# Strided attention on one core: casts, transposes, exps and masked values for two groups at a time

## Chip, cores, metric

One core of one Trainium2 chip. The metric is the device time of one execution in microseconds (us). Times inside a profile count from the start of its span, which is some 1.7 us shorter than the timed execution. A run over 1.5% above the fastest of its kernel counts as slow here, and ratios use the other runs ("fast") alone.

## The reference

Every query attends to the 16 keys at positions 0, 64, 128 and so on.

```python
batch, heads, seq, dim = (8, 12, 1024, 64)      # Q, K, V in float32; stride 64
attend_positions = np.arange(0, seq, stride)    # 16 positions, the same for every query
scores  = np.einsum('bhqd,bhkd->bhqk', q, k) * scale       # scale = 1/sqrt(dim)
weights = np.exp(scores - max); weights /= weights.sum() + 1e-10
result  = np.einsum('bhqk,bhkd->bhqd', weights, v)
```

Q and the result are 25.2 MB each. Only a sixteenth of K and V is read (0.39 MB each).

## The kernel before

The 96 heads form 24 groups of 4. A group's way: load Q (1024 KB), cast it to bf16 on GpSimd (POOL), transpose it on VectorE (DVE), four score matmuls on TensorE (PE), two exps on ScalarE (ACT), then eight output matmuls in three tiles of 3, 2 and 3. DVE takes the reciprocal of the sums of each tile. It also multiplies tiles 0 and 2; ACT copies tile 1 and POOL multiplies it. At last the group is stored (1024 KB). All loads and stores are issued to one queue (q1 of the page: 51.12 of 51.19 MB) in program order. In the timelines every engine starts its instructions in program order, and in the traces all 50 transfers land in the order of their issue. In the names below, qn is a loaded Q tile, qb its bf16 copy, qt the transposed copy, sc the scores, w the exps, v the masked values and o_ps the outputs in PSUM; "lead" is how many groups ahead of its outputs a step runs.

```python
QBUFS = 8; OBUFS = 9
# qb, qt, rec, score tile (1 bank), output tile (3 banks): 2 buffers each
def cast(g):      nc.gpsimd.tensor_copy(out=qb[g], in_=qn[g])                    # 128x2048
def transpose(g): nc.vector.transpose(qt[g].bitcast(I32), qb[g].bitcast(I32))
def scores(g):    # four matmuls into one bank, then two exps into w_bufs[g % 3]
    ...
def outputs(g, c):
    i0, n = ((0, 3), (3, 2), (5, 3))[c]
    ...           # n matmuls, then:
    nc.vector.reciprocal(r, ps[:, 0:n, 4 * D : 4 * D + 4])
    if n == 3:
        nc.vector.tensor_tensor(out=to, in0=o, in1=by, op=ALU.mult)
    else:
        nc.scalar.copy(to, o)
        nc.gpsimd.tensor_tensor(out=to, in0=to, in1=by, op=ALU.mult)
...
def ahead(g):
    transpose(g + 2); scores(g + 1); values(g + 2); cast(g + 3)     # limits at NG cut

for g in range(NG):
    if g > 0:
        ahead(g)              # the work of later groups stands before the outputs of g
    for c in range(3):
        outputs(g, c)
    if g == 0:
        ahead(g)
    ...                       # keys and values of later groups
    store(g)
    if g + QBUFS < NG:
        load(g + QBUFS)
```

So a cast runs three groups ahead of its outputs, a transpose two and the scores one.

The softmax here doesn't subtract the row's maximum and nothing guards it: scores larger than these inputs give would overflow.

Of the kernel before, what the change touches and what calls it, by code (L numbers as in the profile page):

```python
# [11 lines left out]
FP32 = mybir.dt.float32  # L12
BF16 = mybir.dt.bfloat16
I16 = mybir.dt.int16
I32 = mybir.dt.int32
# [4 lines left out]
def _ap_with(ap: bass.AP, new_ap, extra_offset: int = 0) -> bass.AP:  # L20
    return dataclasses.replace(
        ap, ap=[list(p) for p in new_ap], offset=ap.offset + extra_offset
    )


def _copy(nc, out: bass.AP, in_: bass.AP):

    sides = [
        mybir.BassSymbolicTensorAccessPattern(
            ap=side.ap, dtype=side.dtype, bass_ap=side,  # L30
            is_dma=True, for_custom_bir_dma=True,
        )
        for side in (in_, out)
    ]
    return nc.sync.add_instruction(  # L35
        mybir.InstDMACopy(
            name=nc.get_next_instruction_name(), engine=mybir.EngineType.SP,
            ins=sides[:1], outs=sides[1:], queue="qSPDynamicHW",
            mode="Copy",
        )  # L40
    )
# [5 lines left out]



@with_exitstack  # L50
def kernel(
    ctx: ExitStack,
# [7 lines left out]
    nc = tc.nc  # L60

    B, H, S, D = Q.shape
    NK = S // stride
    scale = 1.0 / math.sqrt(D)

    P = 128
    HG = 4
    NG = B * H // HG
    NC = NG // 2
    SD = S * D  # L70
    KW = P + NK
    assert B * H == NG * HG and S == 1024 and D == 64 and NK == 16
    QBUFS = 8
    OBUFS = 9

    const = ctx.enter_context(tc.tile_pool(name="const", bufs=1))
    qn_pool = ctx.enter_context(tc.tile_pool(name="qn", bufs=QBUFS))
    out_pool = ctx.enter_context(tc.tile_pool(name="outsb", bufs=OBUFS))
    qb_pool = ctx.enter_context(tc.tile_pool(name="qb", bufs=2))
    qt_pool = ctx.enter_context(tc.tile_pool(name="qt", bufs=2))  # L80
    rec_pool = ctx.enter_context(tc.tile_pool(name="rec", bufs=2))
    psum_sc = ctx.enter_context(tc.tile_pool(name="psc", bufs=2, space=bass.MemoryType.PSUM))
    psum_o = ctx.enter_context(tc.tile_pool(name="po", bufs=2, space=bass.MemoryType.PSUM))

    ctx.enter_context(tc.manual_schedule())
# [5 lines left out]
    qn = {}  # L91

    def load(g):
        qn[g] = qn_pool.tile([P, 32 * D], FP32, name="qn", tag="qn")
        n = P if g < 2 else 32
        _copy(nc, qn[g], _ap_with(Q, [[HG * SD // n, n], [1, HG * SD // n]], g * HG * SD))

    nc.sync.dma_start(k_raw, _ap_with(K, kv_src))
    load(0)
    nc.sync.dma_start(v_raw, _ap_with(V, kv_src))  # L100
    for g in range(1, QBUFS):
        load(g)


# [2 lines left out]
    id_v = identity.rearrange("p (c b a k) -> p c b a k", c=2, b=2, a=2)  # L107
# [5 lines left out]
    col4 = const.tile([P, 4], I16, name="col4")  # L113
    nc.gpsimd.iota(col4, pattern=[[1, 4]], base=0, channel_multiplier=0)
    for c in range(2):
        for a in range(2):
            for e in range(2):
                nc.gpsimd.tensor_copy(  # L118
                    out=perm_v[:, c, a, :, e], in_=id_v[:, c, :, a]
                )  # L120

    k_t = const.tile([P, NG, 2, KW], BF16, name="k_t")
    nc.vector.memset(k_t[:, 0:8], 0.0)  # L123
    w_bufs = []
    for i in range(3):
        w = const.tile([P, 8, P], BF16, name=f"w{i}")
        nc.vector.memset(w, 0.0)  # L127
        w_bufs.append(w)
    nc.gpsimd.memset(k_t[:, 8:NG], 0.0)  # L129
# [10 lines left out]
        out=s_sel, in0=col4, scalar1=slot_f, scalar2=None, op0=ALU.is_equal  # L140
    )
    v_bufs = []
    for i in range(3):
        v = const.tile([P, 4 * D + 4], BF16, name=f"v{i}")
        nc.vector.tensor_copy(out=v[:, 4 * D :], in_=s_sel)
        v_bufs.append(v)
    mask = const.tile([P, 4, D], BF16, name="mask")
    nc.vector.tensor_copy(out=mask, in_=s_sel.unsqueeze(2).to_broadcast([P, 4, D]))
# [7 lines left out]
    def key_rows(m):  # L156
        part = slice(4 * m, 4 * m + 4)
        nc.scalar.copy(k_bf[:, part], k_raw[:, part])  # L158
        nc.vector.transpose(  # L159
            k_r[:, part].rearrange("p n d -> p (n d)").bitcast(I32),  # L160
            k_bf[:, part].rearrange("p n d -> p (n d)").bitcast(I32),
        )
# [12 lines left out]


    def value_rows(n):
        for c in range(2):
            vp = psum_sc.tile([P, NC // 2, D], FP32, name="vp", tag="sc")
            nc.tensor.matmul(  # L180
                vp, lhsT=perm_v[:, c].rearrange("p a b e k -> p (a b e k)"),
                rhs=v_bf[:, 6 * n : 6 * n + 6], start=True, stop=True,
            )
            nc.vector.tensor_copy(out=v_rep[:, 6 * n : 6 * n + 6, c], in_=vp)  # L184

    qb, qt, wt, vb, rec, out_sb = {}, {}, {}, {}, {}, {}


    def values(g):
        vb[g] = v_bufs[g % 3]  # L190
        nc.gpsimd.tensor_tensor(  # L191
            out=vb[g][:, 0 : 4 * D].rearrange("p (s d) -> p s d", s=4), in0=mask,
            in1=v_rep[:, g // 2, g % 2].unsqueeze(1).to_broadcast([P, 4, D]),
            op=ALU.mult,
        )

    def cast(g):
        qb[g] = qb_pool.tile([P, 32 * D], BF16, name="qb", tag="qb")
        nc.gpsimd.tensor_copy(out=qb[g], in_=qn[g])  # L199

    def transpose(g):
        qt[g] = qt_pool.tile([P, 32 * D], BF16, name="qt", tag="qt")
        nc.vector.transpose(qt[g].bitcast(I32), qb[g].bitcast(I32))  # L203

    def scores(g):
        sc = psum_sc.tile([P, 512], FP32, name="sc", tag="sc")
        q = qt[g]
        for e in range(2):
            for f in range(2):
                nc.tensor.matmul(  # L210
                    sc, lhsT=k_t[:, g, f, NK * (1 - e) : NK * (1 - e) + P],
                    rhs=_ap_with(
                        q, [q.ap[0], [D, 8], [16 * D, 2], [2, 32]],
                        extra_offset=8 * D * e + f,
                    ),
                    start=e + f == 0, stop=e + f == 2,
                )
        w = wt[g] = w_bufs[g % 3]
        for a in range(2):
            wa = w[64 * a : 64 * a + 64]  # L220
            nc.scalar.activation(  # L221
                out=_ap_with(wa, [wa.ap[0], [P, 8], [1, 2], [2, 32]], extra_offset=64 * a),
                in_=sc[64 * a : 64 * a + 64].rearrange("p (t x q) -> p t x q", t=8, x=2),
                func=AF.Exp, bias=0.0, scale=scale,
            )


    def outputs(g, c):
        if c == 0:
            out_sb[g] = out_pool.tile([P, 4, 8, D], FP32, name="out_sb", tag="out_sb")  # L230
            rec[g] = rec_pool.tile([P, 8, 4], FP32, name="rec", tag="rec")
        i0, n = ((0, 3), (3, 2), (5, 3))[c]
        ps = psum_o.tile([P, 3, 512], FP32, name="o_ps", tag="o")
        for i in range(n):
            nc.tensor.matmul(  # L235
                ps[:, i, 0 : 4 * D + 4], lhsT=wt[g][:, i0 + i], rhs=vb[g],
                start=True, stop=True,
            )
        r = rec[g][:, i0 : i0 + n]
        o = ps[:, 0:n, 0 : 4 * D].rearrange("p i (s d) -> p i s d", s=4)  # L240
        to = out_sb[g][:, :, i0 : i0 + n].rearrange("p s i d -> p i s d")
        by = r.unsqueeze(3).to_broadcast([P, n, 4, D])
        nc.vector.reciprocal(r, ps[:, 0:n, 4 * D : 4 * D + 4])  # L243
        if n == 3:
            nc.vector.tensor_tensor(out=to, in0=o, in1=by, op=ALU.mult)  # L245
        else:
            nc.scalar.copy(to, o)  # L247
            nc.gpsimd.tensor_tensor(out=to, in0=to, in1=by, op=ALU.mult)  # L248

    def store(g):  # L250
        o = out_sb[g]
        _copy(
            nc,
            _ap_with(out, [[16 * D, P], [2 * SD, 2], [1, 16 * D]], g * HG * SD),
            _ap_with(o, [o.ap[0], [1, 1], [1, 32 * D]]),
        )

    key_rows(0)
    cast(0)
    cast(1)  # L260
    keys(0, 0)
    transpose(0)
    scores(0)
    keys(0, 1)
    nc.vector.tensor_copy(out=v_bf, in_=v_raw)
    transpose(1)
    value_rows(0)
    values(0)
    values(1)
    cast(2)  # L270
    def ahead(g):
        if g + 2 < NG:
            transpose(g + 2)
        if g + 1 < NG:
            scores(g + 1)
        if g + 2 < NG:
            values(g + 2)
        if g + 3 < NG:
            cast(g + 3)

    for g in range(NG):
        if g > 0:
            ahead(g)
        for c in range(3):
            outputs(g, c)
        if g == 0:
            ahead(g)
        if g in (1, 5):
            key_rows(g // 4 + 1)
        if g in (2, 3, 6, 7):  # L290
            keys(g // 4 + 1, g % 4 - 2)
        if g == 4:
            value_rows(1)
        store(g)
        if g + QBUFS < NG:
            load(g + QBUFS)
# [1 line left out]
_INS = ['Q', 'K', 'V', 'stride']  # L298
_OUTS = [((8, 12, 1024, 64), 'float32')]
# [30 lines left out]
```

## Time and profile before

| | before |
|---|---|
| time, median of 3 | 129.21 us (129.09 to 131.93, a slow run) |
| span of the profiled run | 127.6 us |
| DMA queue busy | 96.7% of the span |
| DVE, POOL, PE, ACT busy | 75%, 71%, 53%, 45% |
| last store issued | 119.9 us |

The rows of digits in the prediction below are the page's slices: the span in 40 equal parts, busy share in tenths. Lines such as "20.57 0.63 SPq ..." are DMA issues: start, duration, and what is moved. Lines of groups end with "busy us, mean ns of one | idle time of the engine before them and who ended it". "Half clock" (also "cold") names what the traces show: four score matmuls take 1.86 to 1.92 us instead of 1.06, and the granted clock in the traces' records is 0.5 instead of 1. These records begin at 24.8 us before and at 29.9 us in the changed kernel; ahead of that the PEclk row and the means over a stretch count a full clock that nothing measured.

### The profile page before, as it was taken

The page shows a single profiled execution, that of the slowest core. Times are in us where ns is not written, and L with a number is a line of the kernel's source. Part 1 is how long each engine was busy: PE and PEld are TensorE (multiplying, and loading weights), DVE is VectorE, ACT ScalarE, POOL GpSimd, SP SyncE. Part 2 cuts the span into 40 slices and gives each one's busy share as a digit, 9 for nine tenths or more (in the row PEclk, how much of TensorE's full clock was granted, in tenths as well). Part 3 has the DMA queues.
Part 4 walks back from the last instruction along what each step waited for, and adds up shares of the span by engine and source line. Part 5 has one row for each costly group of instructions (what it writes and reads, how often), then busy time and mean ns, then how long its engine had stood idle before and what let it go on. Part 6 is the DMA issues. An engine that isn't in the chain of part 4 may idle for free.

```text
span 127.6 us, 1150 instructions
## 1 busy us (share of the span) xinstructions
PE 67.2 (53%) x292; PEld 30.1 (24%) x292; DVE 95.5 (75%) x167; ACT 57.5 (45%) x96; POOL 90.3 (71%) x89
## 2 busy tenths in 40 slices
PE   0005267766456796436757565379734877365100
PEld 0002032233222343212423232124221433132000
DVE  6947557788898678898879888897889878977300
ACT  4110614576771458776445653543554626462100
POOL 8962489877898286898888888898689887433300
PEclk9999999999955558999756999955999657998555
DMA  2999989898998998999989989999999999999980
GB/s 68 378 319 468 462 360 483 349 483 362 460 465 352 480 455 339 506 385 393 501 344 447 460 375 450 426 403 457 442 380 455 439 393 421 424 426 424 429 360 26
DMA packets 7910, 51.19 MB, mean 401 GB/s; under 512 B 3872, under 2 KB 3872, under 8 KB 3872
## 3 DMA queue, kind: packets, MB, share of 16 engines
q1 hardware_dynamic: 7904, 51.12, 96.7%
q8 instruction: 2, 0.03, 0.1%
q14 instruction: 4, 0.03, 0.1%
HBM read 25.95 MB, written 25.17 MB: 401 GB/s over the span
## 4 chain that ended last, share of the span: by engine, by line
DVE 48%; DMA 16%; PE 14%; issue 9%; POOL 4%; SPq 1%; ACT 0%; DVEq 0%; POOLq 0%
DVE out_sb L245 30%; PE o_ps L235 11%; DVE qt L203 10%; DMA out_dram<-out_sb 9%; DMA qn<-in_Q_dram 7%; DVE rec L243 7%; PE sc L210 3%; POOL out_sb L248 2%; POOL qb L199 1%; DVE v_rep L184 1%; SPq L35 1%; POOL v L191 1%; ACT out_sb L247 0%; SPq L100 0%; DVE k_r L159 0%
## 5 line engine op out<-in xcount | busy, mean ns | idle before, releaser
L235 PE MATMUL o_ps<-v,w 128*128 128x260 bf16 x192 | 40.0, 333 | 36.1 <-DVE out_sb L245 34.5
L221 ACT ACTIVATE w<-sc 64x512 bf16<-64x512 f32 x48 | 35.3, 735 | 30.1 <-PE sc L210 28.3
L199 POOL CAST qb<-qn 128x2048 bf16<-128x2048 f32 x24 | 45.3, 1889 | 4.2 <-DMA qn<-in_Q_dram 4.2
L245 DVE TENSOR_TENSOR out_sb<-o_ps,rec 128x768 f32<-128x768 f32 x48 | 46.0, 958 | 1.7
L248 POOL TENSOR_TENSOR out_sb<-out_sb,rec 128x512 f32<-128x512 f32 x24 | 25.0, 1042 | 22.2 <-ACT out_sb L247 22.2
L210 PE MATMUL sc<-qt,k_t 128*128 128x512 bf16 x96 | 33.3, 479 | 12.8 <-DVE qt L203 11.6
L235 PEld LDWEIGHTS <-w 128*128 128x128 bf16 x192 | 18.7, 113 | 63.5 <-DVE out_sb L245 48.1
L203 DVE STREAM_TRANSPOSE qt<-qb 128x1024 int32<-128x1024 int32 x24 | 29.6, 1233 | 4.7 <-POOL qb L199 4.7
L243 DVE RECIPROCAL rec<-o_ps 128x12 f32<-128x12 f32 (+1 forms) x72 | 15.3, 212 | 15.9 <-PE o_ps L235 15.8
L247 ACT COPY out_sb<-o_ps 128x512 f32<-128x512 f32 x24 | 14.0, 585 | 24.9 <-DVE rec L243 12.1
L191 POOL TENSOR_TENSOR v<-mask,v_rep 128x256 bf16<-128x256 bf16 x24 | 16.0, 669 | 2.3 <-DVE v_rep L184 2.3
L210 PEld LDWEIGHTS <-k_t 128*128 128x128 bf16 x96 | 10.8, 113 | 23.8 <-issue 10.7
L169 ACT COPY k_t<-k_r 32x128 bf16<-32x128 bf16 x20 | 5.9, 295 | 2.2 <-DVE k_r L159 1.9
L129 POOL MEMSET k_t<- 128x4608 bf16 x1 | 3.9, 3937 | 0.0
L180 PE MATMUL vp<-v_bf,perm_v 128*128 128x384 bf16 x4 | 1.8, 513 | 2.4 <-DVE v_rep L184 2.4
L139 DVE TENSOR_SCALAR s_sel<-col,slot_f 128x4 bf16<-128x4 int16 x1 | 2.5, 2546 | 0.1
L158 ACT CAST k_bf<-k_raw 128x256 bf16<-128x256 f32 x3 | 1.2, 405 | 3.1 <-DMA k_raw<-in_K_dram 3.0
L184 DVE CAST v_rep<-vp 128x384 bf16<-128x384 f32 x4 | 2.1, 543 | 0.6 <-PE vp L180 0.6
L123 DVE MEMSET k_t<- 128x1152 uint32 x1 | 1.0, 1018 | 1.0 <-PEq L311 1.0
L158 ACT ACT_TABLE_LOAD x1 | 1.3, 1283 | 0.7 <-PEq L311 0.7
L127 DVE MEMSET w<- 128x512 uint32 x3 | 1.5, 485 | 0.2
L118 POOL COPY perm_v<-identity 128x32 bf16<-128x32 bf16 x8 | 1.2, 209 | 0.0
(16 smaller groups left out, 5.0 us busy)
## 6 DMA issues: line engine op xcount, KB each, us to landing
qn<-in_Q_dram SPq DMA_DIRECT2D x24, 1024.0 KB, 11.7
out_dram<-out_sb SPq DMA_DIRECT2D x24, 1024.0 KB, 9.8
k_raw<-in_K_dram SPq DMA_DIRECT2D x1, 384.0 KB, 4.3
v_raw<-in_V_dram SPq DMA_DIRECT2D x1, 384.0 KB, 7.3
```

Source lines behind the costliest of these rows:

```text
L129: nc.gpsimd.memset(k_t[:, 8:NG], 0.0)
L169: op(k_t[dst : dst + 32, 8 * m + c : 8 * m + 8 : 2, :, col : col + NK], k_r[src : src + 32, 4 * m : 4 * m + 4].rearrange("p n (a k f) -> p ...
L191: nc.gpsimd.tensor_tensor(out=vb[g][:, 0 : 4 * D].rearrange("p (s d) -> p s d", s=4), in0=mask, in1=v_rep[:, g // 2, g % 2].unsqueeze(1).t ...
L199: nc.gpsimd.tensor_copy(out=qb[g], in_=qn[g])
L203: nc.vector.transpose(qt[g].bitcast(I32), qb[g].bitcast(I32))
L210: nc.tensor.matmul(sc, lhsT=k_t[:, g, f, NK * (1 - e) : NK * (1 - e) + P], rhs=_ap_with(q, [q.ap[0], [D, 8], [16 * D, 2], [2, 32]], extra_ ...
L221: nc.scalar.activation(out=_ap_with(wa, [wa.ap[0], [P, 8], [1, 2], [2, 32]], extra_offset=64 * a), in_=sc[64 * a : 64 * a + 64].rearrange( ...
L235: nc.tensor.matmul(ps[:, i, 0 : 4 * D + 4], lhsT=wt[g][:, i0 + i], rhs=vb[g], start=True, stop=True,)
L243: nc.vector.reciprocal(r, ps[:, 0:n, 4 * D : 4 * D + 4])
L245: nc.vector.tensor_tensor(out=to, in0=o, in1=by, op=ALU.mult)
L247: nc.scalar.copy(to, o)
L248: nc.gpsimd.tensor_tensor(out=to, in0=to, in1=by, op=ALU.mult)
```

## The change

The intent is to pay the fixed part of an instruction once for two groups (170 ns of a transpose, by the 303 ns for 128 columns and 1233 for 1024 in the trace of before). A pair's Q tile is 128x4096. One cast, one transpose, one masked-values multiply and two exps serve both groups, and the score tile has two banks, one for each group. To start early, the first three pairs go group by group. In exchange there are five Q pairs (ten loads up front), eight output tiles, one qb pair and one score tile.

```diff
-    QBUFS = 8
-    OBUFS = 9
+    QBUFS = 5          # pairs
+    OBUFS = 8
-    qb_pool ... bufs=2          psum_sc ... bufs=2
+    qb_pool ... bufs=1          psum_sc ... bufs=1     (tiles of two groups)
...
+    def cast(n, h=slice(0, 2)):
+        ...
+        nc.gpsimd.tensor_copy(out=qb[n][:, h], in_=qn[n][:, h])
...
     for n in range(NC):
         g = 2 * n
         outputs(g, 0)
         outputs(g, 1)
+        if n == 0:
+            transpose(1, one)
+            group_weights(2)            # scores and exps of one group
+            values(1)
+            cast(1, two)
+        ...                             # n == 1 alike
+        elif 2 < n < NC - 1:
+            scores(g + 2)
+            scores(g + 3)
+            weights(n + 1)              # exps of a pair
+            if n + 2 < NC:
+                transpose(n + 2)
+            if n + 3 < NC:
+                cast(n + 3)
         outputs(g, 2)
         store(g)
+        if n == 2:
+            transpose(3)
+            scores(6)
+            scores(7)
+            weights(3)
+            cast(4)
         outputs(g + 1, 0)
         ...
         store(g + 1)
+        if n == 2:
+            transpose(4)
+            cast(5)
+        if n + 2 < NC:
+            values(n + 2)
```

The work for later groups now stands in the middle of a group's outputs, and from pair 3 on a cast runs three pairs ahead and a transpose two.

More of the change, by code (lines that the diff above doesn't have):

```diff
@@ L70 @@
     SD = S * D
+    QW = 32 * D
+    VW = 4 * D + 4
     KW = P + NK
     assert B * H == NG * HG and S == 1024 and D == 64 and NK == 16
-    QBUFS = 8
-    OBUFS = 9
+    QBUFS = 5
+    OBUFS = 8
     const = ctx.enter_context(tc.tile_pool(name="const", bufs=1))
@@ L78 @@
     out_pool = ctx.enter_context(tc.tile_pool(name="outsb", bufs=OBUFS))
-    qb_pool = ctx.enter_context(tc.tile_pool(name="qb", bufs=2))
+    qb_pool = ctx.enter_context(tc.tile_pool(name="qb", bufs=1))
     qt_pool = ctx.enter_context(tc.tile_pool(name="qt", bufs=2))
-    rec_pool = ctx.enter_context(tc.tile_pool(name="rec", bufs=2))
-    psum_sc = ctx.enter_context(tc.tile_pool(name="psc", bufs=2, space=bass.MemoryType.PSUM))
+    rec_pool = ctx.enter_context(tc.tile_pool(name="rec", bufs=4))
+    psum_sc = ctx.enter_context(tc.tile_pool(name="psc", bufs=1, space=bass.MemoryType.PSUM))
     psum_o = ctx.enter_context(tc.tile_pool(name="po", bufs=2, space=bass.MemoryType.PSUM))
@@ L93, in load @@
     def load(g):
-        qn[g] = qn_pool.tile([P, 32 * D], FP32, name="qn", tag="qn")
+        if g % 2 == 0:
+            qn[g // 2] = qn_pool.tile([P, 2, QW], FP32, name="qn", tag="qn")
         n = P if g < 2 else 32
-        _copy(nc, qn[g], _ap_with(Q, [[HG * SD // n, n], [1, HG * SD // n]], g * HG * SD))
+        _copy(
+            nc, qn[g // 2][:, g % 2],
+            _ap_with(Q, [[HG * SD // n, n], [1, HG * SD // n]], g * HG * SD),
+        )
     nc.sync.dma_start(k_raw, _ap_with(K, kv_src))
@@ L100 @@
     nc.sync.dma_start(v_raw, _ap_with(V, kv_src))
-    for g in range(1, QBUFS):
+    for g in range(1, 2 * QBUFS):
         load(g)
@@ L115 @@
     for c in range(2):
-        for a in range(2):
-            for e in range(2):
-                nc.gpsimd.tensor_copy(
-                    out=perm_v[:, c, a, :, e], in_=id_v[:, c, :, a]
-                )
+        for e in range(2):
+            nc.gpsimd.tensor_copy(
+                out=perm_v[:, c, :, :, e],
+                in_=id_v[:, c].rearrange("p b a k -> p a b k"),
+            )
     k_t = const.tile([P, NG, 2, KW], BF16, name="k_t")
@@ L124 @@
     w_bufs = []
-    for i in range(3):
-        w = const.tile([P, 8, P], BF16, name=f"w{i}")
+    for i in range(2):
+        w = const.tile([P, 16, P], BF16, name=f"w{i}")
         nc.vector.memset(w, 0.0)
@@ L142 @@
     v_bufs = []
-    for i in range(3):
-        v = const.tile([P, 4 * D + 4], BF16, name=f"v{i}")
-        nc.vector.tensor_copy(out=v[:, 4 * D :], in_=s_sel)
+    for i in range(2):
+        v = const.tile([P, 2, VW], BF16, name=f"v{i}")
+        nc.vector.tensor_copy(
+            out=v[:, :, 4 * D :], in_=s_sel.unsqueeze(1).to_broadcast([P, 2, 4])
+        )
         v_bufs.append(v)
@@ L177, in value_rows @@
     def value_rows(n):
+        vp = psum_o.tile([P, 3, 512], FP32, name="vp", tag="o")
+        part = slice(6 * n, 6 * n + 6)
         for c in range(2):
-            vp = psum_sc.tile([P, NC // 2, D], FP32, name="vp", tag="sc")
             nc.tensor.matmul(
-                vp, lhsT=perm_v[:, c].rearrange("p a b e k -> p (a b e k)"),
-                rhs=v_bf[:, 6 * n : 6 * n + 6], start=True, stop=True,
-            )
-            nc.vector.tensor_copy(out=v_rep[:, 6 * n : 6 * n + 6, c], in_=vp)
@@ L186 @@
-    qb, qt, wt, vb, rec, out_sb = {}, {}, {}, {}, {}, {}
-    def values(g):
-        vb[g] = v_bufs[g % 3]
+                vp[:, c, 0 : 6 * D], lhsT=perm_v[:, c].rearrange("p a b e k -> p (a b e k)"),
+                rhs=v_bf[:, part], start=True, stop=True,
+            )
+        nc.vector.tensor_copy(
+            out=v_rep[:, part].rearrange("p n c d -> p c n d"),
+            in_=vp[:, 0:2, 0 : 6 * D].rearrange("p c (n d) -> p c n d", n=6),
+        )
+    qb, qt, wt, vb, sc, rec, out_sb = {}, {}, {}, {}, {}, {}, {}
@@ L191, in values @@
+    def values(n):
+        vb[n] = v_bufs[n % 2]
         nc.gpsimd.tensor_tensor(
-            out=vb[g][:, 0 : 4 * D].rearrange("p (s d) -> p s d", s=4), in0=mask,
-            in1=v_rep[:, g // 2, g % 2].unsqueeze(1).to_broadcast([P, 4, D]),
+            out=vb[n][:, :, 0 : 4 * D].rearrange("p h (s d) -> p h s d", s=4),
+            in0=mask.unsqueeze(1).to_broadcast([P, 2, 4, D]),
+            in1=v_rep[:, n].unsqueeze(2).to_broadcast([P, 2, 4, D]),
             op=ALU.mult,
         )
-    def cast(g):
-        qb[g] = qb_pool.tile([P, 32 * D], BF16, name="qb", tag="qb")
-        nc.gpsimd.tensor_copy(out=qb[g], in_=qn[g])
@@ L201, in transpose @@
-    def transpose(g):
-        qt[g] = qt_pool.tile([P, 32 * D], BF16, name="qt", tag="qt")
-        nc.vector.transpose(qt[g].bitcast(I32), qb[g].bitcast(I32))
+    def cast(n, h=slice(0, 2)):
+        if n not in qb:
+            qb[n] = qb_pool.tile([P, 2, QW], BF16, name="qb", tag="qb")
+        nc.gpsimd.tensor_copy(out=qb[n][:, h], in_=qn[n][:, h])
+    def transpose(n, h=slice(0, 2)):
+        if n not in qt:
+            qt[n] = qt_pool.tile([P, 2, QW], BF16, name="qt", tag="qt")
+        nc.vector.transpose(
+            qt[n][:, h].rearrange("p h d -> p (h d)").bitcast(I32),
+            qb[n][:, h].rearrange("p h d -> p (h d)").bitcast(I32),
+        )
@@ L205, in scores @@
     def scores(g):
-        sc = psum_sc.tile([P, 512], FP32, name="sc", tag="sc")
-        q = qt[g]
+        n, h = divmod(g, 2)
+        if h == 0:
+            sc[n] = psum_sc.tile([P, 2, 512], FP32, name="sc", tag="sc")
+        q = qt[n]
         for e in range(2):
@@ L210, in scores @@
                 nc.tensor.matmul(
-                    sc, lhsT=k_t[:, g, f, NK * (1 - e) : NK * (1 - e) + P],
+                    sc[n][:, h], lhsT=k_t[:, g, f, NK * (1 - e) : NK * (1 - e) + P],
                     rhs=_ap_with(
                         q, [q.ap[0], [D, 8], [16 * D, 2], [2, 32]],
-                        extra_offset=8 * D * e + f,
+                        extra_offset=h * QW + 8 * D * e + f,
                     ),
@@ L217, in scores, with weights @@
                 )
-        w = wt[g] = w_bufs[g % 3]
+    def weights(n, h0=0, hn=2):
+        w = wt[n] = w_bufs[n % 2]
         for a in range(2):
@@ L221, in scores @@
             nc.scalar.activation(
-                out=_ap_with(wa, [wa.ap[0], [P, 8], [1, 2], [2, 32]], extra_offset=64 * a),
-                in_=sc[64 * a : 64 * a + 64].rearrange("p (t x q) -> p t x q", t=8, x=2),
+                out=_ap_with(
+                    wa, [wa.ap[0], [P, 8 * hn], [1, 2], [2, 32]],
+                    extra_offset=64 * a + 8 * P * h0,
+                ),
+                in_=sc[n][64 * a : 64 * a + 64, h0 : h0 + hn].rearrange(
+                    "p h (t x q) -> p (h t) x q", t=8, x=2
+                ),
                 func=AF.Exp, bias=0.0, scale=scale,
@@ L228, in outputs @@
     def outputs(g, c):
+        n, h = divmod(g, 2)
         if c == 0:
@@ L231, in outputs @@
             rec[g] = rec_pool.tile([P, 8, 4], FP32, name="rec", tag="rec")
-        i0, n = ((0, 3), (3, 2), (5, 3))[c]
+        i0, m = ((0, 3), (3, 2), (5, 3))[c]
         ps = psum_o.tile([P, 3, 512], FP32, name="o_ps", tag="o")
-        for i in range(n):
+        for i in range(m):
             nc.tensor.matmul(
-                ps[:, i, 0 : 4 * D + 4], lhsT=wt[g][:, i0 + i], rhs=vb[g],
+                ps[:, i, 0:VW], lhsT=wt[n][:, 8 * h + i0 + i], rhs=vb[n][:, h],
                 start=True, stop=True,
             )
-        r = rec[g][:, i0 : i0 + n]
-        o = ps[:, 0:n, 0 : 4 * D].rearrange("p i (s d) -> p i s d", s=4)
-        to = out_sb[g][:, :, i0 : i0 + n].rearrange("p s i d -> p i s d")
-        by = r.unsqueeze(3).to_broadcast([P, n, 4, D])
-        nc.vector.reciprocal(r, ps[:, 0:n, 4 * D : 4 * D + 4])
-        if n == 3:
+        r = rec[g][:, i0 : i0 + m]
+        o = ps[:, 0:m, 0 : 4 * D].rearrange("p i (s d) -> p i s d", s=4)
+        to = out_sb[g][:, :, i0 : i0 + m].rearrange("p s i d -> p i s d")
+        by = r.unsqueeze(3).to_broadcast([P, m, 4, D])
+        nc.vector.reciprocal(r, ps[:, 0:m, 4 * D : VW])
+        if m == 3:
             nc.vector.tensor_tensor(out=to, in0=o, in1=by, op=ALU.mult)
@@ L254, in store, with group_weights @@
             _ap_with(out, [[16 * D, P], [2 * SD, 2], [1, 16 * D]], g * HG * SD),
-            _ap_with(o, [o.ap[0], [1, 1], [1, 32 * D]]),
+            _ap_with(o, [o.ap[0], [1, 1], [1, QW]]),
         )
+        if g + 2 * QBUFS < NG:
+            load(g + 2 * QBUFS)
+    def group_weights(g):
+        scores(g)
+        weights(g // 2, g % 2, 1)
+    one, two = slice(0, 1), slice(1, 2)
     key_rows(0)
-    cast(0)
-    cast(1)
     keys(0, 0)
-    transpose(0)
-    scores(0)
+    cast(0, one)
@@ L264 @@
+    transpose(0, one)
     keys(0, 1)
+    group_weights(0)
+    cast(0, two)
     nc.vector.tensor_copy(out=v_bf, in_=v_raw)
-    transpose(1)
     value_rows(0)
     values(0)
-    values(1)
-    cast(2)
-    def ahead(g):
-        if g + 2 < NG:
-            transpose(g + 2)
-        if g + 1 < NG:
-            scores(g + 1)
-        if g + 2 < NG:
-            values(g + 2)
-        if g + 3 < NG:
-            cast(g + 3)
-    for g in range(NG):
-        if g > 0:
-            ahead(g)
-        for c in range(3):
-            outputs(g, c)
-        if g == 0:
-            ahead(g)
-        if g in (1, 5):
-            key_rows(g // 4 + 1)
-        if g in (2, 3, 6, 7):
-            keys(g // 4 + 1, g % 4 - 2)
-        if g == 4:
+    transpose(0, two)
@@ new lines @@
+    group_weights(1)
+    cast(1, one)
+    for n in range(NC):
+        g = 2 * n
+        outputs(g, 0)
+        outputs(g, 1)
+        if n == 0:
[3 more added lines that the diff above has]
+            cast(1, two)
+        elif n == 1:
+            transpose(2, one)
+            group_weights(4)
+            cast(2, two)
+        elif 2 < n < NC - 1:
[6 more added lines that the diff above has]
+                cast(n + 3)
+        outputs(g, 2)
+        store(g)
+        if n == 2:
[4 more added lines that the diff above has]
+            cast(4)
+        outputs(g + 1, 0)
+        outputs(g + 1, 1)
+        if n == 0:
+            transpose(1, two)
+            group_weights(3)
+            cast(2, one)
+        elif n == 1:
+            transpose(2, two)
+            group_weights(5)
+            cast(3)
+        outputs(g + 1, 2)
+        store(g + 1)
+        if n == 2:
[3 more added lines that the diff above has]
+            values(n + 2)
+        if n in (0, 4):
+            key_rows(n // 4 + 1)
+        if n in (1, 2, 5, 6):
+            keys(n // 4 + 1, n % 4 - 1)
+        if n == 2:
@@ L293 @@
             value_rows(1)
-        store(g)
-        if g + QBUFS < NG:
-            load(g + QBUFS)
 _INS = ['Q', 'K', 'V', 'stride']
```

## The prediction

> **What bounds the kernel now.** I read the page's slices and queue line first.
>
> ```profile
> DVE  6947557788898678898879888897889878977300
> ...
> POOL 8962489877898286898888888898689887433300
> PEclk9999999999955558999756999955999657998555
> DMA  2999989898998998999989989999999999999980
> ...
> q1 hardware_dynamic: 7904, 51.12, 96.7%
> ```
>
> The reader is to see that the DMA row is full from the second slice to the last but one, while no compute row is. The queue was busy 96.7% of 127.6 us = 123.4 us; only 4.2 us are free, at the two ends. The bytes don't change, so 123.4 us plus those ends is a floor: nothing in this change can win 2%.
>
> Then the busy time by stretch, because the totals hide how near the compute is to this floor (columns: us, busy us and instructions of each engine, clock, DMA share, GB/s).
>
> ```profile
> 25.20:62.00 36.80, 22.02 (x103) 10.25 (x104) 30.23 (x55) 22.32 (x43) 28.02 (x24) 0.81 1.00 422
> 62.00:99.00 37.00, 22.98 (x106) 10.52 (x104) 31.81 (x54) 17.95 (x27) 31.39 (x27) 0.82 1.01 428
> 99.00:120.00 21.00, 12.81 (x59) 5.69 (x59) 16.77 (x30) 9.38 (x14) 12.04 (x12) 0.77 1.01 424
> ```
>
> DMA is saturated in all three, at about 424 GB/s: a 1024 KB transfer costs 2.47 us, a group (load and store) 4.94 us.
>
> The DMA issues in order of time say how far ahead of that the compute is:
>
> ```profile
> 20.57 0.63 SPq L35 DMA_DIRECT2D out_dram<-out_sb  x1
> ...
> 27.36 0.59 SPq L35 DMA_DIRECT2D out_dram<-out_sb  x1
> ...
> 46.58 0.59 SPq L35 DMA_DIRECT2D out_dram<-out_sb  x1
> ...
> 92.61 27.79 SPq L35 DMA_DIRECT2D out_dram<-out_sb  x8
> ```
>
> These are stores 0, 1, 5, and 16 to 23 (the last issued at 119.9 in the view of the output tensor). Ledger: by 9.6 us the slices' rates (68, 378, 319 GB/s over 3.2 us each) make 2.45 MB, of which K and V are 0.79. The rest of eight loads, 6.7 MB, takes till 25.5 us. Allowing some 0.5 us for issue (my choice), store g must be issued by 25 + 4.94 g up to g = 16, later ones 2.47 us apart: store 23 by 121.3. It came at 119.9. **So DMA bounds it, but compute has 1.4 us of slack at the end**; between, up to 11 us (store 16: 92.6 against 104).
>
> [...] the transposes agree: 303 ns for 128 columns, 1233 for 1024, so 1.038 ns a column and 170 fixed. [...] the 32-element POOL copies take 209 ns, which agrees with some 180 fixed. [...] four score matmuls take 1.86 us at 21.7 and 1.06 at 25.9. (The clock row's nines before 25 us are thus not the granted clock.)
>
> **The change, part by part.**
>
> ```profile
> L199 POOL CAST qb<-qn 128x2048 bf16<-128x2048 f32 x24 | 45.3, 1889 | 4.2 <-DMA qn<-in_Q_dram 4.2
> L245 DVE TENSOR_TENSOR out_sb<-o_ps,rec 128x768 f32<-128x768 f32 x48 | 46.0, 958 | 1.7
> L221 ACT ACTIVATE w<-sc 64x512 bf16<-64x512 f32 x48 | 35.3, 735 | 30.1 <-PE sc L210 28.3
> L203 DVE STREAM_TRANSPOSE qt<-qb 128x1024 int32<-128x1024 int32 x24 | 29.6, 1233 | 4.7 <-POOL qb L199 4.7
> ```
>
> *Removed:* fixed parts. Paired transpose 170 + 2048 x 1.038 = 2.30 us (saves 0.17 a pair); paired cast 180 + 2 x 1709 ns = 3.60 (saves 0.18); masked values 180 + 2 x 489 ns = 1.16 (saves 0.18)[...]. DVE per pair: 4 x 0.958 + 6 reciprocals (1.27) + 2.30 = 7.40, plus one wait of some 0.3 for the third output tile = 7.85 with semaphores, 3.93 a group against 4.09 now (view of the chain, for instance 52.11 to 56.19). At half clock eight score matmuls take 3.8 us instead of 2.1 and outlast the transpose: about 9.5. With a third of the time at half clock, 8.4 a pair. All this beats 9.88 of DMA and is off the end-setting path, if it starts in time.
>
> *Moved:* two more loads go up front. So store g is due by 30 + 4.94 g up to g = 14, then 2.47 apart: store 23 again by 121.4.
>
> *Added:* waits at the start. I walk the program order with the rows above.
>
> Group 0: scores stay at 10.9 to 12.7. Value rows, their copy and the paired values end near 15.8. Then PE does scores(1) *before* outputs(0,0): 15.8 + 1.9, outputs at 18.5, DVE to 19.95. Transpose of group 2 (1.25), its scores (1.9 cold) and outputs(0,2) (0.85) now stand *before* the last third of group 0: **store 0 near 25.3**, not 20.6. Due 30: hidden.
>
> Groups 1 to 3: each has, in series, reciprocal and multiply 1.2, reciprocal 0.2, transpose 1.25, scores 1.06, outputs(g,2) 0.5, reciprocal and multiply 1.2 = 5.6 with gaps (before, scores ran beside other work). Store 3 near 42 (due 44.8). At half clock 6.8: 46.
>
> Groups 4 to 6: store 4 near 45.5. Then the paired transpose 2.3, eight scores 2.1, outputs 0.5, then group 5's work of 3 us: store 5 at 53.5 (due 54.7). Then transpose(4) 2.3, v_rep 0.95, a third of group 6 1.4; transpose(5) must wait for cast(5), which with a **single qb buffer** begins only after transpose(4) (55.3 + 3.6 = 58.9), then 2.3 and 1.2: **store 6 near 62.5, due 59.7: DMA dry for some 3 us**, and it isn't refilled. At half clock store 5 is at 59 and store 6 at 68: 8 us dry.
>
> Rest: store 7 at 65.9, seven pairs at 7.85 to 8.4, then 5.8 for the last, which has no transpose: store 23 at 126.7 to 130.6, instead of 119.9. From there to the end took 7.7 us before; with no queue left 7.2. Span 133.9 to 137.8; the timed median was 1.6 above the span: **135.5 to 139.4**; with a cold start about 143.
>
> **Rivals.** *Hidden after all:* the start's delay fits in the two extra loads, which give 5 us. For it: stores 0 to 5 are in time even by my walk. Then 129 to 130.5. Against it: the tail. Load 23 would land two stores earlier (106.3 - 4.9 = 101.3), but its cast is now three pairs ahead of its outputs, not three groups: cast to 104.9, transpose to 107.2, then the rest of group 18 and five groups of 2.9 us plus scores without cover (2.1): store 23 near 124.8, 3.4 late, 132.5. *POOL becomes the bound* (3.60 + 2 x 1.04 + 1.16 = 6.84 a pair, and transpose to cast to transpose is 5.9 in a ring): both under 7.85, so only at pairs 4 and 5. *ACT or the single score tile stalls PE:* exps of a pair end some 5 us before the next scores; no. *Faster:* the floor of 123.4 forbids it beyond about 1%.
>
> **Range and chances.** Walk: 135.5 to 139.4, clock about +4, hidden cases 129 to 132.5 for errors in my walk, which assumes that halves of a tile don't wait for each other. I take 137, range 130.5 to 143. Slower needs over 131.8, 2.6 us of delay; the walk finds 6 or more and two separate reasons: 0.84. Same 0.14, faster 0.02.
>
> **What would show it.** Right: store 0 near 25 us, store 6 later than 60 and a dip in the DMA row near 60 us (slices 19 to 21); DMA share of the span under 94%; last store issue beyond 125; paired transpose 2.3 us, cast 3.6; DVE waiting for PE in groups 1 to 5. Wrong: a DMA row full throughout and a last store by 122 (then the start was hidden), or a transpose(5) that doesn't wait for its cast. What would make it wrong: PE warm from the start and other overlaps that my walk missed, or coarser waits between the halves, which would make it slower still.

## The result

The changed kernel took **141.85 us** (median of 4, 140.97 to 142.37) against 129.45 for the kernel before in the same rounds: ratio 1.0961, 95% interval 1.0873 to 1.1049. A ratio here is the mean of one kernel's fast runs over the mean of the other's of the same rounds, so not quite the ratio of the medians. The forecast of "slower" and its range, 130.5 to 143, held; its 137 was 4.9 us too low.

The page of the changed kernel, the rows that were shown of before:

```profile
DVE  6935463655638806959888989897767658567630
...
POOL 8755829475279381499979598494692693712320
PEclk9999999997777755558689999959995599599555
DMA  3999999999979989590999999979999999928874
...
q1 hardware_dynamic: 7904, 51.12, 90.7%
```

A slice is now 3.49 us. The DMA row has two holes, around 57 and 65 us, and it thins out in the last five slices. The queue was busy 90.7% of 139.6 us = 126.6 us, so 13.0 us were free instead of 4.2.

The DMA issues of the changed kernel in order of time (stores 0, 1, 4, 5, 6, 7, and the last ten, of which the last was issued at 133.9):

```profile
24.59 0.63 SPq L35 DMA_DIRECT2D out_dram<-out_sb  x1
...
30.79 0.59 SPq L35 DMA_DIRECT2D out_dram<-out_sb  x1
...
46.16 0.59 SPq L35 DMA_DIRECT2D out_dram<-out_sb  x1
...
56.44 0.59 SPq L35 DMA_DIRECT2D out_dram<-out_sb  x1
...
65.44 0.59 SPq L35 DMA_DIRECT2D out_dram<-out_sb  x1
...
68.95 0.59 SPq L35 DMA_DIRECT2D out_dram<-out_sb  x1
...
96.90 37.57 SPq L35 DMA_DIRECT2D out_dram<-out_sb  x10
```

Stores 5 and 6 come 10 and 9 us after the one before them, where the DMA needs 4.94 us a group (2 x 1024 KB at the 424 GB/s measured before). That is the two holes.

What the paired instructions cost (groups of the changed kernel, shapes kept apart):

```profile
L215 POOL CAST qb<-qn 128x4096 bf16<-128x4096 f32 x9 | 32.4, 3596 | 14.4 <-DVE rec L273 7.0 <-DVE qt L220 5.4 <-DMA qn<-in_Q_dram 2.0
...
L245 ACT ACTIVATE w<-sc 64x1024 bf16<-64x1024 f32 x18 | 23.4, 1301 | 17.5 <-PE sc L232 17.3
L220 DVE STREAM_TRANSPOSE qt<-qb 128x2048 int32<-128x2048 int32 x9 | 20.6, 2290 | 5.7 <-POOL qb L215 5.7
```

The savings are there. A paired transpose takes 2.29 us against 2 x 1.23, a cast 3.60 against 2 x 1.89. In all, DVE is busy 93.1 us instead of 95.5 and POOL 86.9 instead of 90.3. Both engines do less and end 14 us later.

Where do the 14 us arise? The table gives the end of each group's last DVE multiply, read from the traces (us). "No later loads" are the experiments e1 and e2 below.

| group | before | changed | before, no later loads | changed, no later loads |
|---|---|---|---|---|
| 0 | 20.5 | 24.5 | 20.9 | 24.6 |
| 3 | 35.7 | 43.1 | 36.1 | 43.3 |
| 4 | 40.1 | 46.1 | 40.5 | 46.2 |
| 6 | 50.8 | 65.4 | 51.2 | 65.2 |
| 8 | 59.0 | 73.3 | 59.4 | 73.3 |
| 17 | 96.6 | 109.3 | 97.0 | 107.6 |
| 23 | 119.8 | 133.9 | 120.2 | 130.8 |

By group 6 the changed kernel is 14.6 us late: 4.0 in group 0, 3.4 in groups 1 to 3, -1.4 in group 4, 8.6 in groups 5 and 6. Groups 7 to 23 take 68.5 us against 69.0, so the pairs gain next to nothing there. Without later loads these take 65.6, 3.4 us less than before, and waits for loads take 2.9 of it back. But not all of the 3.4 us is a gain of pairing: three groups' transposes (3 x 1.23 = 3.7 us of DVE) had been done ahead in groups 5 and 6. Groups 8 to 15, in which both kernels transpose eight groups, show the gain itself: 31.7 us against 33.4 without later loads, some 0.4 us a pair. Group 7, the second half of a pair and without a transpose of its own, gives another 1.1. The last eight groups give only 0.5, though two paired transposes are left there against six single ones.

The worst stretch is the change from groups to pairs. The timeline of the changed kernel (start, duration, instruction, and in brackets the idle time before it and who ended it):

```profile
46.02 2.30 DVE L220 STREAM_TRANSPOSE qt<-qb 128x2048 int32<-128x2048 int32 x1
...
48.38 3.59 PE L232 MATMUL sc<-qt,k_t 128*128 128x512 bf16 x8 [3.54 <-DVE qt L220]
48.38 3.60 POOL L215 CAST qb<-qn 128x4096 bf16<-128x4096 f32 x1 [2.26 <-DVE qt L220]
...
52.66 0.23 DVE L273 RECIPROCAL rec<-o_ps 128x12 f32<-128x12 f32 x1 [4.34 <-PE o_ps L265]
...
58.32 3.60 POOL L215 CAST qb<-qn 128x4096 bf16<-128x4096 f32 x1 [1.91 <-DVE qt L220]
...
61.95 2.31 DVE L220 STREAM_TRANSPOSE qt<-qb 128x2048 int32<-128x2048 int32 x1 [1.60 <-POOL qb L215]
```

DVE transposes pair 3 and then has nothing to do for 4.34 us. PE must first run eight scores at half clock (3.59 us; at 76.59 us eight took 1.96) and only then the outputs of group 5. At 58.32 POOL casts pair 5 as soon as the transpose of pair 4 has freed the only qb tile, and DVE waits 1.60 us for it. Meanwhile the queue runs dry. Stretch by stretch (columns: us, busy us and instructions of PE, weight loads, DVE, ACT and POOL, granted clock, DMA share, GB/s), the changed kernel:

```profile
46.00:67.00 21.00, 13.12 (x42) 5.20 (x42) 13.69 (x18) 7.90 (x11) 13.15 (x7) 0.59 0.77 295
```

and the kernel before:

```profile
46.00:67.00 21.00, 12.75 (x62) 5.98 (x61) 17.89 (x32) 12.55 (x23) 17.51 (x16) 0.83 1.01 424
```

A DMA share of 0.77 over 21 us is 4.8 us lost, and DVE did 13.7 us of work instead of 17.9.

At the end, the last two transposes of the changed kernel wait for casts:

```profile
102.58 2.31 DVE L220 STREAM_TRANSPOSE qt<-qb 128x2048 int32<-128x2048 int32 x1 [1.54 <-POOL qb L215]
...
113.09 2.31 DVE L220 STREAM_TRANSPOSE qt<-qb 128x2048 int32<-128x2048 int32 x1 [2.56 <-POOL qb L215]
```

The chain that ended last has the second of these casts (start, duration, what):

```profile
109.46 3.60 POOL qb L215
113.07 0.02 issue
113.09 2.31 DVE qt L220
```

These casts wait for loads. The waits view puts theirs down to a DVE reciprocal that ends at the same moment, but a cast needs no reciprocal, and the trace's landing records have the loads 21 and 23 landing at 98.8 and 109.3 us, each 0.15 us before its cast begins (98.95 and 109.46).

### The profile page after: what moved, and what is told of

It is laid out like the page before. It is cut to its first block, busy times and chain, and to the rows that moved or that the text cites. A ratio compares the mean times of both kernels' runs of the same rounds, so it can differ in the third digit from the quotient of the medians.

```text
span 139.6 us, 1078 instructions
## 1 busy us (share of the span) xinstructions
PE 73.4 (53%) x292; PEld 30.0 (21%) x292; DVE 93.1 (67%) x154; ACT 54.6 (39%) x78; POOL 86.9 (62%) x64
## 3 DMA queue, kind: packets, MB, share of 16 engines
q1 hardware_dynamic: 7904, 51.12, 90.7%
## 4 chain that ended last, share of the span: by engine, by line
DVE 30%; DMA 22%; PE 19%; POOL 15%; issue 7%; ACT 1%; SPq 1%; POOLq 0%; DVEq 0%
DVE out_sb L275 14%; DMA qn<-in_Q_dram 13%; PE sc L232 12%; DVE qt L220 11%; POOL qb L215 11%; DMA out_dram<-out_sb 9%; PE o_ps L265 6%; DVE rec L273 4%; POOL out_sb L278 3%; ACT w L245 1%; POOL v L204 1%; DVE v_rep L194 1%; PE vp L190 0%; SPq L35 0%; SPq L105 0%
## 5 line engine op out<-in xcount | busy, mean ns | idle before, releaser
L215 POOL CAST qb<-qn 128x4096 bf16<-128x4096 f32 (+1 forms) x15 | 43.7, 2914 | 18.2 <-DVE rec L273 7.0
L232 PE MATMUL sc<-qt,k_t 128*128 128x512 bf16 x96 | 36.2, 534 | 24.8 <-DVE qt L220 24.8
L245 ACT ACTIVATE w<-sc 64x1024 bf16<-64x1024 f32 (+1 forms) x30 | 32.2, 1074 | 35.3 <-PE sc L232 35.0
L273 DVE RECIPROCAL rec<-o_ps 128x12 f32<-128x12 f32 (+1 forms) x72 | 15.4, 214 | 27.8 <-PE o_ps L265 27.8
L220 DVE STREAM_TRANSPOSE qt<-qb 128x2048 int32<-128x2048 int32 (+1 forms) x15 | 27.9, 1857 | 8.0 <-POOL qb L215 8.0
L265 PEld LDWEIGHTS <-w 128*128 128x128 bf16 x192 | 18.0, 112 | 57.7 <-DVE out_sb L275 41.3
L232 PEld LDWEIGHTS <-k_t 128*128 128x128 bf16 x96 | 11.4, 124 | 43.0 <-issue 20.9
L204 POOL TENSOR_TENSOR v<-mask,v_rep 128x512 bf16<-128x512 bf16 x12 | 13.9, 1155 | 0.9 <-DVE v_rep L194 0.7
L194 DVE CAST v_rep<-vp 128x768 bf16<-128x768 f32 x2 | 1.9, 938 | 1.5 <-PE vp L190 1.5
L134 DVE MEMSET w<- 128x1024 uint32 x2 | 1.8, 912 | 0.3 <-issue 0.3
L146 DVE TENSOR_SCALAR s_sel<-col,slot_f 128x4 bf16<-128x4 int16 x1 | 1.5, 1530 | 0.1
L168 DVE STREAM_TRANSPOSE k_r<-k_bf 128x128 int32<-128x128 int32 x3 | 0.9, 305 | 0.1
```

The lines of the kernel that those rows point to most:

```text
L204: nc.gpsimd.tensor_tensor(out=vb[n][:, :, 0 : 4 * D].rearrange("p h (s d) -> p h s d", s=4), in0=mask.unsqueeze(1).to_broadcast([P, 2, 4, D]),
L215: nc.gpsimd.tensor_copy(out=qb[n][:, h], in_=qn[n][:, h])
L220: nc.vector.transpose(qt[n][:, h].rearrange("p h d -> p (h d)").bitcast(I32), qb[n][:, h].rearrange("p h d -> p (h d)").bitcast(I32),)
L232: nc.tensor.matmul(sc[n][:, h], lhsT=k_t[:, g, f, NK * (1 - e) : NK * (1 - e) + P], rhs=_ap_with(q, [q.ap[0], [D, 8], [16 * D, 2], [2, 32] ...
L245: nc.scalar.activation(out=_ap_with(wa, [wa.ap[0], [P, 8 * hn], [1, 2], [2, 32]], extra_offset=64 * a + 8 * P * h0,), in_=sc[n][64 * a : 6 ...
L265: nc.tensor.matmul(ps[:, i, 0:VW], lhsT=wt[n][:, 8 * h + i0 + i], rhs=vb[n][:, h], start=True, stop=True,)
```

## The experiments

The theory has two parts. The **order** of the start makes every group late: scores before outputs, no overlap in groups 1 to 3, and the change to pairs with one qb. And the compute path sets the end, with only 1.4 us of slack (the time by which it could be later without the DMA waiting), so delay anywhere in it should come out whole. The rivals are: fewer or paired buffers; a steady loop slowed by one score tile; DMA gaps that cost by themselves; late loads in the tail; PE's clock.

All kernels gave correct results, except the three without later loads. Their outputs are wrong, which doesn't matter for the times.

### e1 and e2: the compute path alone

Loads after the first eight (before) or ten (changed) are dropped; later groups reuse the first Q tiles. One execution each.

```diff
-            load(g + QBUFS)
+            qn[g + QBUFS] = qn[g]
```

> The kernel before without the sixteen loads after the first eight (later groups reuse the first Q tiles; the result is wrong on purpose). It shows the compute path alone. My theory: the compute of before needs almost the time it took beside the DMA, since its chain waited for loads under 5 us: last store issued at 117 to 119.5 us (119.9 with loads), span 123 to 125. If it falls below 115, the loads did hold the kernel before and my ledger of slack is wrong.

> The changed kernel without the fourteen loads after the first ten (wrong on purpose). Theory (start order plus a tail that waits for loads): the start stays late (store 6 issued near 65 us, as with loads), pairs from there take 7.6 to 8.4 us, and the tail no longer waits: last store at 126 to 131 instead of 133.9, span 131 to 136. Rival (paired work with one score tile slows the steady state): pairs take over 8.6 us and the last store comes no earlier than 133. Rival (only the DMA gaps matter): span under 128.

Measured: spans of 125.5 and 136.2 us, each a little over its range. The stores of each, first and last issue (e1, then e2):

```profile
L35 SPq DMA_DIRECT2D out_dram<-out_sb x24: 538/539/623, 21.0 to 120.2; - x24
```

```profile
L35 SPq DMA_DIRECT2D out_dram<-out_sb x24: 538/539/636, 24.7 to 130.8; - x24
```

With a third less to move, the kernel before issues its last store at 120.2, just as with all loads (119.9, so a hair outside what I expected). Its compute path needs that time anyway. From the last store to the end took 7.7 us with all loads and takes 5.3 here; that is all that the full queue added. **The kernel before is bound twice, by DMA (read from its queue, 96.7% busy) and by a compute path that ends at nearly the same moment (shown by e1).** The changed path is 10.6 us longer by itself. Its pairs, groups 8 to 15, take 31.7 us for four = 7.9 each, inside the 7.6 to 8.4 expected, so the rival of a slow steady loop falls. Late loads are worth 133.9 - 130.8 = 3.1 us on top; this last number compares single runs in which PE's clock fell differently (the eight scores of pair 10 took 3.62 us at 108.06 in e2 and 2.96 at 109.75 with loads), so by my estimate from that difference it is good to perhaps 1 us.

### e3: the tiles and buffers of the change, the order of before

```diff
+    def ahead(g):
+        transpose half (g + 2); group_weights(g + 1); values of a pair; cast half (g + 3)
     for g in range(NG):          # the loop of the kernel before, all 24 groups
```

> The tiles and buffers of the changed kernel (paired tiles, one qb pair, one two-bank score tile, five Q pairs, eight output tiles, paired masked values), but the order of the kernel before throughout: casts, transposes and exps group by group, scores of the next group beside the outputs of this one. Theory (order of the work): back to 128.5 to 131 us, DMA row full, store 0 near 20.5 us. Rival (fewer or paired buffers): stays over 135.

Measured: 129.52 us, ratio 0.9996 (0.996 to 1.0032). Its page:

```profile
DMA  2999989898998999989989999999999899999980
```

The row is full again; store 0 was issued at 21.46 us, a microsecond later than I expected. Ten loads up front, eight output tiles, one qb pair, one score tile and the paired masked values cost nothing and win nothing in this order. **The loss lies in the order and the pairing of the work**, with what the fewer buffers cost in that order alone (e5).

### e4: only the start undone

Groups 0 to 5 in the order of before; pair 3 is a passage that I had to write (two transposes and casts by halves, then by pairs); the paired loop from pair 4 on is unchanged.

> The changed kernel with only its start undone: groups 0 to 5 in the order of before, pair 3 as a passage, the paired loop unchanged from pair 4 on. Theory with two causes: DMA no longer runs dry near 56 to 67 us, load 23 lands some 5 to 7 us earlier (near 102 to 104), but the tail stays about 25 us from that landing to the last store: 132 to 136 us, faster than 141.85 by 6 to 9. If the start was the only cause: 128.5 to 131. If the start was harmless: over 139.

Measured: 135.42 us, ratio 1.0467 (1.0416 to 1.0519), so 6.4 us better than the change. The DMA row has no hole in the middle any more:

```profile
DMA  3999998998999899899899899899899969828873
```

Still it is 6 us slower than before. Group 6 ends at 50.8 us, exactly as before, but groups 7 and 8, now at the passage, take 16.5 us instead of 8.2:

```profile
63.90 2.31 DVE L220 STREAM_TRANSPOSE qt<-qb 128x2048 int32<-128x2048 int32 x1 [2.47 <-POOL qb L215]
```

So the 8.6 us of groups 5 and 6 moved to groups 7 and 8 (8.3). The passage from a short lead to a long one costs this much in both places where I have seen it, transposes done ahead included. (PE's granted clock changed with the start: 0.75 from 25.2 to 62 us and 0.74 from 62 to 99, against 0.70 and 0.88 in the changed kernel. So this run does not part order from PE's clock; e8 and e10 do.) And it was not the dry queue as such: here the queue stayed full until the tail (DMA share 1.00 from 25.2 to 62 us and 1.02 from 62 to 99, then 0.76) and the time was still lost, because the path had no slack.

### e5: two qb pairs, without later loads

> The changed kernel without later loads (wrong on purpose, as e2) and with two qb pair buffers in place of one; the memory comes from a fourth of the Q pairs that this run doesn't need. Against e2 (last store 130.8, group 6 done at 65.2 us). Theory of the prediction (with one qb pair the cast of pair 5 waits for the transpose of pair 4, and the transpose of pair 5 for that cast): group 6 done 1.3 to 2 us earlier, last store at 128.5 to 130, the rest of the path as in e2. If the single qb were most of the loss: 4 us or more. If none: unchanged within 0.5.

Measured (one execution, which also loads eight groups at first, not ten): span 133.5, group 6 at 64.0 instead of 65.2 us, last store at 128.3. Of the 1.2 us at group 6, 0.6 was there at group 4 (45.6 instead of 46.2), before the passage: the scores of group 3 happened to take 1.07 us, not 1.89. So the single qb costs some 0.6 us at the passage, under half of what was expected and hardly more than the "none" of the expectation: DVE's wait of 1.6 us for the cast is gone, but 0.97 us of waiting for PE stands in its place. The rest of the 2.5 us I can't tell from the clock.

### e6: one move in the passage

```diff
         if n == 2:
             transpose(3)
+        outputs(g + 1, 0)
+        outputs(g + 1, 1)
+        if n == 2:
             scores(6)
             scores(7)
             weights(3)
             cast(4)
-        outputs(g + 1, 0)
-        outputs(g + 1, 1)
```

> The changed kernel with one move in pair 2: the first two thirds of group 5 stand before the eight scores of pair 3, not after them, so PE can do them under the paired transpose and DVE has work under the scores. The 4.3 us that DVE waited there (48.3 to 52.7) should shrink to 1 to 2. Theory (the compute path sets the end, there is no slack left): the whole of it comes out at the end, 138.5 to 140, less whatever the late casts take back. Rival (DMA running dry near 56 to 67 us costs by itself, the path has slack): no change within 0.7 us.

Measured: 140.21 us, ratio 1.0822 (1.0748 to 1.0896), 1.6 us less than the change, a little short of the range; the two kernels' runs just overlap (139.79 to 141.18 and 140.97 to 142.37). DVE's longest wait here fell only from 4.34 to 3.09 us, because the third output tile of group 5 still stands behind eight scores. In the profiled runs group 5 ended 2.9 us earlier, group 6 1.8 and the last group 1.1. But 0.7 us of each was there at group 4, before the edit's place, since the scores of group 2 happened to run at 1.06 us, not 1.87. The edit's own share is thus 2.2, 1.1 and 0.5 us: DVE now waited 1.00 us for the cast of pair 4, and 1.61 for that of pair 5 much as before. So the gain did not come out whole. The traces alone don't exclude the rival (under 0.7 us); the medians speak against it.

### e7: the later transposes moved behind the outputs

```diff
-            transpose(n + 2); cast(n + 3)        # in the middle of group g, from n = 6 on
...
         store(g + 1)
+        if n >= 6: transpose(n + 2); cast(n + 3)
```

> The changed kernel with the transpose and cast of later pairs moved behind both groups of the pair from pair 6 on, so that finished groups aren't held in DVE's order behind a transpose that waits for a load. Theory (the late loads cost the tail some 3 us, 133.9 against 130.8 without loads): 1 to 3 us are won, but eight scores are no longer covered by the transpose in pairs 7 to 10, which costs 0.7 to 1.2 a pair: net 139.5 to 143. If the tail were a main cause as my prediction's second reason had it (3.4 us alone): below 139.5.

Measured: 147.56 us, ratio 1.1362. A miss on the bad side. The waits for casts in the tail are gone, but PE gets the queries so late that the scores lie bare, at half clock (3.57 us):

```profile
92.86 3.57 PE L232 MATMUL sc<-qt,k_t 128*128 128x512 bf16 x8 [1.82 <-DVE qt L220]
...
97.11 0.23 DVE L273 RECIPROCAL rec<-o_ps 128x12 f32<-128x12 f32 x1 [3.09 <-PE o_ps L265]
```

In the changed kernel a transpose in the middle of the outputs covers the eight scores of the next pair (at 77.66 us it ran beside those of 76.59 to 78.55, and DVE went on at 79.84 without a wait). Without that cover DVE waits 3.09 us here and again at 107.83 us, some three times what I had put down.

### e8 and e10: PE kept busy in its gaps

Matmuls of no use before the scores of groups 1 to 7 (four each, e8) or 2 to 7 (six each, e10); the real scores overwrite their result.

```diff
         q = qt[n]
+        if 1 < g < 8:
+            for _ in range(6):
+                nc.tensor.matmul(sc[n][:, h], lhsT=k_t[:, g, 0, 0:P], rhs=spare[:, 0:512],
+                                 start=True, stop=True)
```

> The changed kernel with four matmuls of no use before the scores of groups 1 to 7, in time in which PE waits for a transpose; their result is overwritten. If PE's half clock at the start comes from its idle gaps, the real scores of groups 2 to 5 fall from 1.87 to 1.06 us, groups 1 to 3 take 5.6 us instead of 6.2, store 6 comes near 61 to 62.5 instead of 65.4, and the time falls by 2 to 4 us to 138 to 140. If the clock doesn't follow activity: unchanged or up to 2 us slower.

> As the run with matmuls of no use, but six each and only before the scores of groups 2 to 7, to keep PE busy longer in its gaps and not to delay group 1. Theory (half clock at the start costs 3 to 5 us of the path): 136.5 to 139, scores of groups 2 to 5 mostly at 1.06 us, store 6 near 61 to 63. If six delay the real scores more than the clock gives back: 139 to 142.

Measured: e8 138.69 us, ratio 1.0571 (1.0476 to 1.0666); e10 139.11 us, ratio 1.0658 (1.0572 to 1.0743). Both scatter by over 2 us from run to run (136.9 to 141.0 and 137.3 to 139.9), with two slow runs each, which the medians include; the means of the fast runs are 137.6 (three) and 138.0 (two). So e10's median lies 0.1 us over its range, its fast runs inside. The page of e8 is from a slow run, so I read e10's. Scores of groups 2 and 4 in the changed kernel, then in e10:

```profile
20.73 1.87 PE L232 MATMUL sc<-qt,k_t 128*128 128x512 bf16 x4 [2.20 <-DVE qt L220]
...
33.50 1.89 PE L232 MATMUL sc<-qt,k_t 128*128 128x512 bf16 x4 [2.33 <-DVE qt L220]
```

```profile
21.30 1.06 PE L239 MATMUL sc<-qt,k_t 128*128 128x512 bf16 x4
...
32.12 1.06 PE L239 MATMUL sc<-qt,k_t 128*128 128x512 bf16 x4 [1.36 <-DVE qt L220]
```

With work in the gaps the scores of groups 2 to 6 take 1.06 us. In the changed kernel those from 15.6 to 35.4 us took 1.86 to 1.89, with gaps of 1.74 to 2.33 us before them; in e10 the gaps before the real scores of groups 2 to 5 are at most 1.36 us, and that of group 6, 2.24 us, left its scores at 1.06. From 20 to 46 us PE was busy 57% of the time in the changed kernel and 63% in e10, at a granted clock of 0.87 and 1.00 (the time ahead of the clock records counted as full). What length of gap or what busy share decides is not shown. Groups 1 to 3 then take 5.3 us each instead of 6.2, and group 6 ends at 61.1 instead of 65.4. Of these 4.3 us, 2.6 arrive at the last group; the fast runs are about 4 us faster than the change's 141.8. So a third of the loss, roughly, comes by way of PE's clock: with the gaps that the new order leaves PE, the scores stayed at 1.86 to 1.89 us, and with these gaps filled they took 1.06.

### e9: the last three casts in halves

> The changed kernel with the casts of the last three pairs (9, 10, 11) in two halves, at the same place in the order: the first half need not wait for the second load, which lands some 5 us later, so a cast ends 1.9 us after that landing instead of 3.6. The transpose's cover of the scores stays (what the tail experiment lost). Theory (late loads cost the tail 3 us): DVE's waits for the casts of pairs 10 and 11 (1.5 and 2.6 us) shrink by 1.7 each at most, 0.7 to 2.5 us are won: 139.3 to 141.2. If the late loads cost nothing at the end: 141.9, within 0.5.

Measured: 140.21 us (median of 6, 139.79 to 141.03), ratio 1.0827 (1.0778 to 1.0875), so some 1.6 us less than the change, inside the range. Its intervals and those of the change barely touch. DVE's two waits:

```profile
101.86 2.31 DVE L220 STREAM_TRANSPOSE qt<-qb 128x2048 int32<-128x2048 int32 x1 [0.62 <-POOL qb L215]
...
112.02 2.31 DVE L220 STREAM_TRANSPOSE qt<-qb 128x2048 int32<-128x2048 int32 x1 [2.21 <-POOL qb L215]
```

They shrank by 0.92 and 0.35 us, though in the profiled runs the last group ends only 0.4 us earlier. The late loads are thus a real part of the loss; that it is all of e2's 3 us is not shown.

No version here beats the kernel before, and none that moves the same bytes at this rate can do so by much: its queue is busy for 123.4 of 127.6 us.

## Why the prediction was right

- **The floor and the slack.** Right. e1 shows that compute ends at 120.2 us even with a third less traffic. That is why a late path showed in the time.
- **Store 0 near 25.3.** 24.6.
- **Groups 1 to 3, 5.6 us each, or 6.8 at half clock.** 6.2, with scores at half clock in most of them (1.87 to 1.89 us, the last 1.52); 5.3 with scores at 1.06 us (e10).
- **Stores 5 and 6 at 53.5 and 62.5, or 59 and 68; 3 or 8 us dry.** 56.4, 65.4 and 4.8 us: in the middle of my two cases. The granted clock from 46 to 67 us was 0.59.
- **The single qb delays the transpose of pair 5.** The wait is there, 1.60 us in the trace, but removing it won only some 0.6 (e5).
- **Pairs at 7.85 to 8.4.** 7.9 without later loads.
- **Last store at 126.7 to 130.6.** 130.8 without later loads, 133.9 with them. **This is the step that was off.** The walk's own span took a start at full clock (store 7 at 65.9; 68.95 came, so 3 us late) and left out the tail's waits for loads. These it had found, but used only as a reason why "hidden after all" would fail, with load 23 landing on time, at 101.3. The late start makes the loads late too, for each load stands in the queue behind a store: load 23 landed at 109.3. With the prediction's own 23.5 us from there to the last store that gives 132.8, and 133.9 came.
- **Some luck in the time.** From the last store to the end the prediction put 7.2 us; it took 5.7. That took 1.5 us off the error of the last store; without it, by my estimate, 141.85 would have been some 143.3, just over the range. The upper end, 143, was meant for a cold start and not for late loads.
- **Savings.** Transpose 2.30 (2.29), cast 3.60 (3.60), masked values 1.16 (1.155) were right. The paired exp took 1.30 us (1301 ns for 1024 elements, 734 for 512: 1.107 ns an element and 167 fixed, from these two sizes); my estimate had been 0.16 us lower, and no trace showed it. It made little difference (1% of the chain). The 180 ns that the prediction gives POOL as the fixed part of an instruction rests on its 209 ns copies alone; the casts of the changed kernel, 1891 ns for 2048 elements and 3596 for 4096, make 0.833 ns an element and 186 fixed.
- **What would show it.** DMA share under 94% (90.7%), last store beyond 125 (133.9), DVE waiting for PE (27.8 us instead of 15.8). The dip fell on slices 17 and 19, because the span was longer than the one I counted in.
- **Not explained:** all DMA packets together took 126.6 us instead of 123.4, for the same bytes. In the trace 113 of the 3339 packets of 8 KB took over 500 ns, against a median of 311, and 76 of these lie at 58 to 62 and 68 to 70 us, in or just after the holes.

## What to carry to other kernels

When an engine that looks bound (here DMA) and a dependent chain end at nearly the same time, work saved on one alone wins next to nothing, and a delay of the chain beyond its slack is paid for, here 10.6 us of it without any help of late loads: measure the chain alone, for instance without the loads, before touching it. Work on two items at a time saved the fixed part of an instruction, here 0.17 us a transpose, but here it came with a deeper lead, and filling that lead cost some 8.5 us of the chain in both places where it was put (3.7 us of transposes done ahead included). In e7 a transpose that no longer ran beside PE's scores left DVE waiting 3.09 us in each of two pairs, so put work for later beside something that another engine has to do anyway; ask what each engine does during the others' part of every reordered step.
